# Scan rows loaded two chunks at a time, and output projections by 1024 by 512 quarters, in a hybrid decoder trunk

## Chip, core and metric

The program runs on one core of a Trainium2 chip. The metric is the device time of one launch in microseconds (us): 2238.65 us before, the median of three runs (2238.03 to 2240.89).

## What is computed

A trunk of two residual layers on 1024 tokens of width 1024, all in float32. Layer 0 has two mixers side by side, a Mamba-2 scan in 8 chunks of 128 tokens and differential attention in 8 heads; layer 1 is a gated linear recurrence of 16 heads. Each layer ends in one output projection from 2048 to 1024 that is added to the residual.

```python
# layer 0, in two halves of 1024 channels each
z, xBC, dt, q, k, v, g = split(u @ w_in)
a_cs = cumsum(dt * A)                                   # per head, within a chunk
y_diag = ((C B^T) * exp(segsum(a))) X                   # scores of a chunk, then times X
y_off  = (C prev) * exp(a_cs)                           # what earlier chunks hand on
y = y_diag + y_off + xs * D_skip
y_a = rmsnorm(y * silu(z), ssd_norm_w)
y_b = rmsnorm(diff_attention(q, k, v), subln_w) * silu(g)
h = h + concat(y_a, y_b) @ w_out                        # 2048 x 1024
# layer 1
h = h + (rmsnorm(recurrence(q, k, i, f), norm_w) * silu(g)) @ w_out
out = rmsnorm(h, final_norm_w)
```

## The kernel before

**Numbers.** Every projection multiplies split operands: a value is a rounded part `hi` and the rest `lo`, and three products are summed (hi by hi, hi by lo, lo by hi). So 128 tokens by 1024 inputs take 24 matmuls. `mm_cm` (L174) puts channels on partitions, 128 by 512 outputs each; `mm_tm` (L184) puts tokens on partitions, 128 by 256 outputs each. Weights come in blocks of 1024 rows by 256 columns: `_wprep` loads each half raw (L126, 512 KB into one of two `w_raw` slots), casts it to `w_hi` on ScalarE (L132) and subtracts into `w_lo` on VectorE (L133). There are two slots of each, and a block is prepared while the one before it is in use.

**The scan** (`ssd_steps`) runs in four head groups, woven by hand into the projection pieces of the next group: TensorE's order is as written (`manual_schedule`), that of the other queues is set by a scheduler. A piece is 24 matmuls into one of two `pj` banks: per group eight convolution pieces, evicted by ScalarE alone (L426, L427), and four gate pieces, evicted by a tanh on ScalarE (L232, into the one slot `th`) and a product on VectorE (L233). Per chunk, `first(c)` loads a row tile R (L464: cumulative decays of four heads, 128 columns, broadcast to all partitions; three slots), transposes (L466 to L470), subtracts (L482), exponentiates (L484) and multiplies (L485); `second(c)`, two pieces later, multiplies (L502 to L508) and adds up on VectorE. For `y_off` each pair of chunks loads the same decays again in another layout into the one slot `ey` (L523, two DMAs) and exponentiates them (L525). At each odd chunk, ScalarE squares into `th` (L542) and GpSimd adds from there (L544, L547) before the pair is stored (L548).

**The output projection** (`out_proj`) takes the first 1024 inputs (`ya`), then the second (`yb`). The y tiles come through a raw tile (`w_raw`, `th` or `ey`) and are split from there (`load_y`, L694 to L705). The first half runs over four column blocks of 256, each over all eight token tiles; the second runs over half the tokens with four blocks, and again with the same four, so 12 weight blocks are loaded per layer. Sums are evicted by VectorE (L734, L738, L778), squared on ScalarE (L781), and `finish` normalizes 512 tokens at a time.

SP's queue issues nearly all loads and stores, in order: a DMA whose tile is not free yet holds up what stands behind it.

Of the kernel before, what the change touches and what calls it, by code (L numbers as in the profile page):

```python
# [89 lines left out]
class Net:  # L90
# [23 lines left out]
    def _wprep(self, i):  # L114
# [4 lines left out]
        hi = self.t("w_hi", [P, KT, WB], F32R)  # L119
        lo = self.t("w_lo", [P, KT, WB], F32R)  # L120
        for q in range(2):
            raw = self.t("w_raw", [P, KT // 2, WB])
            k0 = q * (KT // 2)
            o = 0
            for c0, n in cols:
                nc.sync.dma_start(  # L126
                    raw[:, :, o:o + n],
                    src[row0 + k0 * P:row0 + (k0 + KT // 2) * P, c0:c0 + n].rearrange(
                        "(k p) n -> p k n", p=P))
                o += n  # L130
# [48 lines left out]
    def mm_tm(self, out, w, uh, ul, ks=range(KT)):  # L179
        nc = self.nc  # L180
        wh, wl = w
        for k in ks:
            for j, (uu, ww) in enumerate(((uh, wh), (uh, wl), (ul, wh))):
                nc.tensor.matmul(out, lhsT=uu[k], rhs=ww[:, k, :],  # L184
                                 start=(k == 0 and j == 0), stop=(k == KT - 1 and j == 2))
# [20 lines left out]
    def proj_v(self, u):  # L206
        vs = []
        run(self.v_pieces(u, vs))
        return self.v_of(vs)

# [242 lines left out]
def ssd_steps(S, g, tiles, ya, at, lag):  # L453
# [4 lines left out]
    X_, sts, eas = {}, {}, {}  # L458

    def first(c):  # L460
        x0, x1, Bt, Ct = tiles[:4]
        cs = slice(c * P, c * P + P)
        R = S.t(("G", "G", "wT")[(8 * g + c) % 3], [P, 4, P])
        nc.sync.dma_start(R, bc(S.acs_d[hs, cs].unsqueeze(0), [P, 4, P]))  # L464
# [15 lines left out]
        nc.vector.tensor_tensor(cb, pt[:, 384:512], S.triu, op=ALU.mult)  # L480
        for h in range(4):
# [4 lines left out]
        X_[c] = pk, R  # L486

    def second(c):
        Ct = tiles[3]
        cs = slice(c * P, c * P + P)  # L490
        pk, sc = X_[c]
# [26 lines left out]
        if c % 2 == 0:  # L518

            c2 = slice(c * P, (c + 2) * P)  # L520
# [5 lines left out]
            eas[c // 2] = ea, S.t("o", [P, 2, 256])  # L526
        ea, tt = (z[:, :, (c % 2) * P:(c % 2) * P + P] for z in eas[c // 2])
# [5 lines left out]
        if c % 2 == 1:  # L533
            t = eas[c // 2][1]
# [6 lines left out]
            sq = S.t("th", [P, 2, 256])  # L541
# [147 lines left out]
def load_y(S, y_d, wcols, hf, k, tags):  # L689

    nc = S.nc
    n = len(tags)
# [3 lines left out]
    for j in range(n):  # L696
        y = S.t(tags[j], [P, 2, 512], F32R)
        if wcols is not None and k < KT:
            w = wcols[:, k + j:k + j + 1]
            nc.scalar.activation(y[:, 0], raw[:, j], AF.Identity, scale=w)  # L700
            nc.vector.scalar_tensor_tensor(y[:, 1], raw[:, j], w, y[:, 0].bitcast(F32),
                                           op0=ALU.mult, op1=ALU.subtract)
        else:
            nc.scalar.copy(y[:, 0], raw[:, j])
            nc.vector.tensor_tensor(y[:, 1], raw[:, j], y[:, 0].bitcast(F32), op=ALU.subtract)  # L705
# [4 lines left out]
def out_proj(S, y_d, wcols, x_d, x1_tags, rs_a, finish):  # L710
# [3 lines left out]
    part = lambda y, t: [[z[:, i, t * P:t * P + P] for z in y] for i in range(2)]  # L714
    load = lambda hf, k, *tags: load_y(S, y_d, wcols, hf, k, tags)
    ya, yb = [[], []], [[], []]
    for hf in range(2):
        for k in range(0, KT, 2):
            ya[hf] += load(hf, k, "u", "u")
    x1s = [], []  # L720
    for cb in range(4):
        w = S.wnext()
        for hf in range(2):
            x1 = S.t(x1_tags[2 * cb + hf], [P, 4, WB])
            nc.sync.dma_start(x1, x_d[hf * 512:hf * 512 + 512, cb * WB:cb * WB + WB].rearrange(
                "(t p) n -> p t n", p=P))
            x1s[hf].append(x1)
            for t2 in range(2):
                pa = S.ps("pj", [P, 2, WB])
                ts_ = slice(2 * t2, 2 * t2 + 2)  # L730
                for t in range(2):
                    S.mm_tm(pa[:, t], w, *part(ya[hf], 2 * t2 + t))
                if rs_a is None:
                    nc.vector.tensor_tensor(x1[:, ts_], pa, x1[:, ts_], op=ALU.add)  # L734
                else:
                    for t in range(2):
                        tok = hf * 4 + 2 * t2 + t
                        nc.vector.scalar_tensor_tensor(x1[:, 2 * t2 + t], pa[:, t], rs_a[:, tok:tok + 1],  # L738
                                                       x1[:, 2 * t2 + t], op0=ALU.mult, op1=ALU.add)
        if cb == 2:  # L740
            for k in range(KT, 2 * KT - 2, 2):
                yb[0] += load(0, k, "A", "A")
    yb[0] += load(0, 2 * KT - 2, "u")
    ws, pbs = {}, {}

    def block(cb, tag):
        ws[cb] = S.wnext()
        if tag == "pj":
            pbs[cb] = [S.ps("pj", [P, 2, WB]) for _ in range(2)]
        elif tag == "big":  # L750
            pb = S.ps("big", [P, 4, WB])
            pbs[cb] = [pb[:, 0:2], pb[:, 2:4]]

# [441 lines left out]
```

## Time and profile before

| | |
|---|---|
| median of three runs | 2238.65 us |
| the profiled execution | 2242.69 us, its span 2240.9 us |
| TensorE busy in the span | 2178.8 us (97%) |
| VectorE, ScalarE, GpSimd busy | 1269.9, 832.2, 188.8 us |

The page reads so: busy time is the union of an engine's instructions; "idle before" is what the engine waited before an instruction, with the instruction that released it behind "<-". PE is TensorE's matmul side, PEld its weight loads, which overlap it; DVE is VectorE, ACT ScalarE, POOL GpSimd, SPq the queue that SP issues. PEclk is the granted TensorE clock as a share of 2.4 GHz; its other level is 1.2 GHz, shown as 0.50.

### The profile page before, as it was taken

Reading aid. Unit: us, or ns where it says so; the run is one execution under the profiler, and the core shown is the slowest. Engines: PE = TensorE matmul, PEld = TensorE weight load, DVE = VectorE, ACT = ScalarE, POOL = GpSimd, SP = SyncE. Lnnn points to the kernel's source line nnn. Section 1 sums busy time; section 2 is a strip of 40 time slices with the busy share of each in tenths; the row PEclk is TensorE's granted clock in tenths of the full one; section 3 lists DMA queues with packets and bytes.
Section 4 is the critical chain, followed back from the end, with each engine's and each line's share of the span. In section 5 each row is a group of like instructions: output and inputs, shape, how many; then the busy total and the mean of one; then the engine's idle time right before and its main releaser. Section 6 shows DMA issues by size and latency. Waiting matters only on the chain.

```text
span 2240.9 us, 40897 instructions
## 1 busy us (share of the span) xinstructions
PE 2178.8 (97%) x16868; PEld 1920.3 (86%) x16868; DVE 1269.9 (57%) x2864; ACT 832.2 (37%) x1903; POOL 188.8 (8%) x216
## 2 busy tenths in 40 slices
PE   6998998899999999999999999999999999999998
PEld 5787776789898988999988989898989898989998
DVE  4765766565656556755453555555555555557444
ACT  4333333234444545644442323232323222324233
POOL 1001111110000000000010010101010101010000
PEclk9999999999999999999999999999999999999999
DMA  4322233332212221525331111111111111125333
GB/s 138 67 84 66 80 85 81 74 81 64 69 36 67 64 69 41 170 66 159 119 104 39 48 48 48 48 48 48 48 48 48 48 49 48 48 67 165 111 103 122
DMA packets 182256, 169.14 MB, mean 75 GB/s; under 512 B 10239, under 2 KB 163233, under 8 KB 182068
## 3 DMA queue, kind: packets, MB, share of 16 engines
q1 hardware_dynamic: 174564, 152.42, 23.1%
q0 software_dynamic: 3280, 9.90, 2.1%
q10 hardware_dynamic: 4224, 4.19, 0.6%
q8 instruction: 132, 2.16, 0.4%
q14 instruction: 56, 0.46, 0.1%
HBM read 132.66 MB, written 25.43 MB: 71 GB/s over the span
## 4 chain that ended last, share of the span: by engine, by line
PE 51%; DMA 1%; ACT 0%; DVE 0%; issue 0%; POOL 0%; POOLq 0%; ACTq 0%
PE pj L174 24%; PE pj L184 14%; PE big L184 5%; PE big L1051 2%; PE big L1139 1%; PE big L1141 1%; PE s L1128 1%; PE big L1093 1%; PE s L1155 1%; PE s L1122 1%; PE big L1087 0%; PE s L159 0%; DMA ey<-yb 0%; DMA th<-in_lvmask 0%; ACT w_hi L132 0%; DVE w_lo L133 0%
## 5 line engine op out<-in xcount | busy, mean ns | idle before, releaser
L174 PE MATMUL pj<-u,w_hi 128*128 128x512 f32 x3072 | 990.0, 400 | 31.3 <-DVE A L233 21.2
L174 PEld LDWEIGHTS pj<-u,w_hi 128*128 128x128 f32 x3072 | 573.4, 190 | 154.7 <-DVE A L233 23.0
L174 PE MATMUL pj<-u,w_lo 128*128 128x512 f32 x1536 | 607.9, 396 | 0.0
L184 PE MATMUL pj<-w_hi,u 128*128 128x256 f32 x2592 | 492.6, 286 | 1.0 <-DVE A L233 1.0
L184 PEld LDWEIGHTS pj<-w_hi,u 128*128 128x128 f32 x2592 | 409.9, 191 | 3.6 <-DVE A L233 1.4
L184 PE MATMUL pj<-w_lo,u 128*128 128x256 f32 x1296 | 368.3, 284 | 0.0
L174 PEld LDWEIGHTS pj<-u,w_lo 128*128 128x128 f32 x1536 | 291.8, 190 | 61.1 <-issue 0.2
L133 DVE TENSOR_TENSOR w_lo<-w_raw,w_hi 128x1024 fp32r<-128x1024 f32 x168 | 206.3, 1251 | 116.9 <-ACT w_hi L132 116.6
L184 PEld LDWEIGHTS pj<-w_lo,u 128*128 128x128 f32 x1296 | 247.8, 191 | 1.0
L132 ACT CAST w_hi<-w_raw 128x1024 fp32r<-128x1024 f32 x168 | 168.1, 1047 | 188.8 <-PE pj L174 107.6
L233 DVE SCALAR_TENSOR_TENSOR A<-th,pj 128x512 f32<-128x512 f32 x80 | 55.1, 689 | 140.9 <-ACT th L232 140.4
L232 ACT ACTIVATE th<-pj 128x512 f32<-128x512 f32 x96 | 57.2, 596 | 208.5 <-PE pj L174 190.8
L617 ACT ACTIVATE p<-p,mx 128x256 f32<-128x256 f32 (+7 forms) x128 | 98.5, 771 | 72.4 <-DVE mx L613 66.4
L148 POOL TENSOR_TENSOR ro<-rs_t,mhalf 128x4 f32<-128x4 f32 x48 | 52.8, 1100 | 682.4 <-DVE rs_t L147 489.1
L603 PE MATMUL big<-A 128*128 128x512 f32 (+3 forms) x384 | 90.3, 352 | 2.6 <-DMA A<-A 1.3
L968 POOL TENSOR_SCALAR A<-th,fN,fB 128x512 f32<-128x512 f32 x32 | 47.6, 1488 | 470.0 <-ACT th L965 470.0
L637 ACT COPY wT<-s 128x512 f32<-128x512 f32 (+2 forms) x96 | 45.8, 477 | 95.8 <-PE s L635 95.1
L639 PE MATMUL s<-V,wT 128*128 128x128 f32 x576 | 79.7, 275 | 0.6 <-ACT wT L637 0.6
L1035 DVE TENSOR_TENSOR A<-A,p 128x512 f32<-128x512 f32 x96 | 65.8, 686 | 23.5 <-PE big L1051 23.0
L639 PEld LDWEIGHTS s<-V,wT 128*128 128x128 f32 x576 | 74.4, 191 | 3.3 <-ACT wT L637 1.1
L1030 DVE TENSOR_TENSOR p<-p,p 128x512 f32<-128x512 f32 x96 | 66.2, 690 | 15.5 <-PE big L1087 6.2
L603 PEld LDWEIGHTS big<-A 128*128 128x128 f32 x384 | 64.5, 189 | 11.3 <-issue 2.3
(330 smaller groups left out, 2977.1 us busy)
## 6 DMA issues: line engine op xcount, KB each, us to landing
w_raw<-in_even_w_in SPq DMA_DIRECT2D x32, 512.0 KB, 4.7
w_raw<-in_odd_w_in SPq DMA_DIRECT2D x64, 256.0 KB, 3.3
w_raw<-in_odd_w_in SPq DMA_DIRECT2D x32, 512.0 KB, 3.9
w_raw<-in_even_w_in SPq DMA_DIRECT2D x48, 256.0 KB, 4.3
w_raw<-in_even_w_out SPq DMA_DIRECT2D x24, 512.0 KB, 4.4
w_raw<-in_odd_w_out SPq DMA_DIRECT2D x24, 512.0 KB, 4.6
A<-A POOLq DMA_DIRECT2D x32, 256.0 KB, 5.5
yo<-ey SPq DMA_DIRECT2D x32, 256.0 KB, 2.0
```

The source lines that it names most:

```text
L132: nc.scalar.copy(hq, raw)
L133: nc.vector.tensor_tensor(lq, raw, hq.bitcast(F32), op=ALU.subtract)
L148: return nc.gpsimd.tensor_tensor(dst, t[:, :n], self.mhalf[:, :n], op=ALU.pow)
L174: nc.tensor.matmul(out, lhsT=ww[:, k, ms], rhs=uu[k][:, sl], start=(n == 0), stop=(n == 3 * KT - 1))
L184: nc.tensor.matmul(out, lhsT=uu[k], rhs=ww[:, k, :], start=(k == 0 and j == 0), stop=(k == KT - 1 and j == 2))
L232: nc.scalar.activation(th, pj, AF.Tanh, scale=0.5)
L233: nc.vector.scalar_tensor_tensor(out, view(th), 1.0, view(pj), op0=ALU.add, op1=ALU.mult)
L603: nc.tensor.matmul(s[:, k0:k0 + kn], lhsT=q[:, isl], rhs=ks[j][:, k0:k0 + kn], start=(j == 0), stop=(j == 1))
L617: nc.scalar.activation(p[:, :n], p[:, :n], AF.Exp, bias=mx, accum_out=z)
L639: nc.tensor.matmul(po[:, i % 4, :], lhsT=wT[:, j * P:j * P + P], rhs=V(j, hh), start=(j == 0), stop=(j == i))
L1030: nc.vector.tensor_tensor(q, q, bc(t0, [P, L // (2 * h), h]), op=ALU.mult)
L1035: nc.vector.tensor_tensor(k, k, bc(halves(Ts[h], 1)[1], [P, L // (2 * h), h]), op=ALU.mult)
```

## The change

The row tile now holds two chunks (256 columns, three slots), and the load for pair i + 1 is issued in `first` of pair i. The second layout is no longer loaded: `first(c)` exponentiates half the heads on each half of the partitions straight from the row tile into `ey` or `cm` (by the chunk's parity), before the subtraction overwrites the rows. The squares go into the chunk's own tile (`p0` or `bt`) in place of `th`. A weight block may now be 512 rows by 512 columns, and the projection runs over quarters of 1024 by 512: two blocks (kq 0 and 1) of 512 rows each, all eight token tiles, sums of 128 by 512. Both weight slots are then in use at once; in the first and the last pair of token tiles the order is kq 0 of both tiles, then kq 1 of both. Eight blocks are loaded per layer. y tiles are loaded into their own second half and split in place.

```diff
+    def rows_load(self, i):
+        if i < 16:
+            g, q = divmod(i, 4)
+            self.rows[i] = self.t(("G", "G", "wT")[i % 3], [P, 4, 256])
+            self.nc.sync.dma_start(self.rows[i], bc(
+                self.acs_d[4 * g:4 * g + 4, q * 256:q * 256 + 256].unsqueeze(0), [P, 4, 256]))
...
     def first(c):
-        R = S.t(("G", "G", "wT")[(8 * g + c) % 3], [P, 4, P])
-        nc.sync.dma_start(R, bc(S.acs_d[hs, cs].unsqueeze(0), [P, 4, P]))
+        if c % 2 == 0:
+            S.rows_load(4 * g + c // 2 + 1)
+        R = S.rows[4 * g + c // 2][:, :, (c % 2) * P:(c % 2) * P + P]
...
+        ea = S.t(("ey", "cm")[c % 2], [P, 2, P])
+        for hh in range(2):
+            nc.scalar.activation(ea[64 * hh:64 * hh + 64], R[64 * hh:64 * hh + 64, hh::2], AF.Exp)
...
     def second(c):
-            ea = S.t("ey", [P, 2, 256])
-            for hh in range(2):
-                nc.sync.dma_start(ea[64 * hh:64 * hh + 64],
-                                  bc(S.acs_d[4 * g + hh:4 * g + 4:2, c2].unsqueeze(0), [64, 2, 256]))
-            nc.scalar.activation(ea, ea, AF.Exp)
...
-            sq = S.t("th", [P, 2, 256])
+            sq = pk[:, 0:512].rearrange("p (b t) -> p b t", b=2)
             nc.scalar.activation(sq, t, AF.Square)
...
 def load_y(S, y_d, wcols, hf, k, tags):
-    raw = S.t("w_raw" if n == 2 else (("th", "ey")[k % 2] if hf else "th"), [P, n, 512])
-    nc.sync.dma_start(raw, y_d(k, n)[:, :, hf * 512:hf * 512 + 512].rearrange("b p t -> p b t"))
+    for j, tag in enumerate(tags):
+        y = S.t(tag, [P, 2, 512], F32R)
+        raw = y[:, 1].bitcast(F32)
+        nc.sync.dma_start(raw, y_d(k + j, 1)[0, :, hf * 512:hf * 512 + 512])
...
 def out_proj(S, y_d, wcols, x_d, x1_tags, rs_a, finish):
+    def pair():
+        i = S.wpos
+        S.wpos += 2
+        S._wprep(i)
+        S._wprep(i + 1)
+        return S.wtiles[i], S.wtiles[i + 1]
+
+    def sums(ws, ys):
+        for t in range(0, NT, 2):
+            pas = [S.ps("pj") for _ in range(2)]
+            order = ((0, 0), (1, 0), (0, 1), (1, 1)) if t in (0, NT - 2) else ((0, 0), (0, 1), (1, 0), (1, 1))
+            for j, kq in order:
+                hf, tt = divmod(t + j, 4)
+                y = ys[hf][4 * kq:4 * kq + 4]
+                S.mm_tm(pas[j], ws[kq], *([z[:, i, tt * P:tt * P + P] for z in y] for i in range(2)),
+                        first=kq == 0, last=kq == 1)
+                if t == NT - 2 and j == 1:
+                    S._wprep(S.wpos + kq)
+                if kq == 1:
+                    yield hf, tt, pas[j]
...
+    for n in range(2):
+        ws = pair()
+        rss = []
+        for hf, t, pa in sums(ws, late):
...
+            xr = x1s[hf, n, t // 2][:, t % 2]
+            nc.vector.tensor_tensor(xr, pa, xr, op=ALU.add)
+            jk = S.t("ey", [P, 512])
+            nc.scalar.activation(jk, xr, AF.Square, accum_out=ss[hf][:, t, n:n + 1])
...
-    out = lambda w: [(w, half * D, [(cb * WB, WB)]) for half in (0, 1, 1) for cb in range(4)]
+    out = lambda w: [(w, kq * 512, [(n * 512, 512)])
+                     for half in (0, 2) for n in range(2) for kq in (half, half + 1)]
```

The scheduler moves what stands around these edits. Three places follow, in the order in which a queue issues; the line numbers are those of each kernel, and a number behind a tile's name tells its copies apart.

**SP's queue early in the scan's first group.** The row loads are L464 before (128 columns) and L219 after (256), the second layout is L523, the store of a finished pair L548 and L558, and L126 and L128 load weights. Before:

```order
L464 DMA G_1258<-acs_d_552 128x4x128
L523 DMA ey_1212<-acs_d_552 64x2x256 x2
L548 DMA ya_74<-o_1049 128x2x256
L464 DMA wT_1335<-acs_d_552 128x4x128
L464 DMA G_1427<-acs_d_552 128x4x128
```

After:

```order
L219 DMA G_1259<-acs_d_552 128x4x256
L558 DMA ya_74<-o_1051 128x2x256
L219 DMA G_1427<-acs_d_552 128x4x256
L128 DMA w_raw_1513<-in_even_w_in 128x4x128 x2
L128 DMA w_raw_1518<-in_even_w_in 128x4x128 x2
L558 DMA ya_74<-o_1217 128x2x256
```

Between two stores of `ya` stood two row loads and two loads of the other layout, the next chunk's rows among them; now one load stands there, for the pair after.

**ScalarE's queue at the first two gate pieces of that group.** The gate's tanh is L232 before and L243 after, the squares L542 and L552, the exponential of the rows L484 and L501, that of the other layout L525 and L497. Before:

```order
L484 ACTIVATE G<-G 128x512
L525 ACTIVATE ey<-ey 128x512
L479 COPY bt<-s_1337 128x128
L438 ACTIVATE p_1255<-A 128x1024
L542 ACTIVATE th<-o 128x512
L232 ACTIVATE th<-pj 128x512 x2
```

After:

```order
L497 ACTIVATE cm<-wT 64x256 x2
L243 ACTIVATE th<-pj 128x512
L501 ACTIVATE wT<-wT 128x4x128
L492 COPY bt<-s_1338 128x128
L449 ACTIVATE p_1256<-A 128x1024
L243 ACTIVATE th<-pj 128x512
L552 ACTIVATE p_1166<-o 128x512
```

Both gate pieces stood behind the squares; now both stand ahead of them.

**VectorE's queue where layer 1's projection passes to its last weight blocks.** The addition of a sum is L778 before and L782 after, the product with the norm's weights L990 and L997, the subtraction for `w_lo` L133 and L135. Before:

```order
L133 TENSOR_TENSOR w_lo_21319<-w_raw_21324,w_hi_21318 128x1024
L778 TENSOR_TENSOR A_20616<-big_21338,A_20616 128x512
L990 TENSOR_TENSOR A_20402<-A_20402,o_20110 128x512
L990 TENSOR_TENSOR A_20616<-A_20616,o_20112 128x512
L778 TENSOR_TENSOR A_20616<-big_21338,A_20616 128x512
L133 TENSOR_TENSOR w_lo_21448<-w_raw_21449,w_hi_21447 128x1024
```

After:

```order
L782 TENSOR_TENSOR A_19518<-pj_20020,A_19518 128x512
L135 TENSOR_TENSOR w_lo_20047<-w_raw_20048,w_hi_20046 128x1024
L135 TENSOR_TENSOR w_lo_20047<-w_raw_20052,w_hi_20046 128x1024
L997 TENSOR_TENSOR A_19518<-A_19518,o_19230 128x512
L782 TENSOR_TENSOR A_19518<-pj_20021,A_19518 128x512
L997 TENSOR_TENSOR A_19518<-A_19518,o_19230 128x512
L135 TENSOR_TENSOR w_lo_20085<-w_raw_20086,w_hi_20084 128x1024
L135 TENSOR_TENSOR w_lo_20085<-w_raw_20090,w_hi_20084 128x1024
```

One block was prepared between two additions of the block before it; now two blocks are prepared around the last two additions (A_19518) of the quarter before.

## Rows read from the trace of the kernel before


**Rows 1.** The page, busy time by engine: us (share of the span) and instructions.

```profile
PE 2178.8 (97%) x16868; PEld 1920.3 (86%) x16868; DVE 1269.9 (57%) x2864; ACT 832.2 (37%) x1903; POOL 188.8 (8%) x216
```

**Rows 2.** Windows: stretch, its us, busy of PE, PEld, DVE, ACT, POOL (count), PEclk, DMA share, GB/s.

```profile
0.00:100.00 100.00, 83.19 (x388) 63.23 (x389) 60.69 (x113) 43.98 (x70) 10.87 (x23) 1.00 0.41 110
100.00:440.00 340.00, 310.27 (x1611) 252.70 (x1610) 214.38 (x440) 115.26 (x192) 40.02 (x50) 0.95 0.30 78
```

**Rows 3.** Windows inside the scan, same columns: where the clock falls.

```profile
160.00:200.00 40.00, 34.00 (x158) 27.20 (x155) 28.26 (x56) 13.14 (x21) 4.28 (x5) 0.91 0.32 86
...
260.00:300.00 40.00, 32.95 (x150) 25.95 (x149) 22.98 (x49) 9.90 (x16) 6.26 (x6) 0.87 0.25 71
...
360.00:420.00 60.00, 44.57 (x216) 35.63 (x214) 28.81 (x67) 15.52 (x26) 8.18 (x9) 0.89 0.24 58
```

**Rows 4.** PE's waits from 100 to 440: waiter, releaser, total, times, longest.

```profile
PE pj L174 <- DVE A L233: 21.2, 7, 5.6
PE pj L174 <- DVE A L570: 8.0, 1, 8.0
```

**Rows 5.** Timeline at a group's first gate piece: start, us, what, [idle before <-releaser].

```profile
266.46 0.61 ACT L542 ACTIVATE th<-o 128x512 f32<-128x512 f32 x1
...
267.15 2.44 POOL L547 TENSOR_TENSOR V<-V,th 128x256 f32<-128x256 f32 x2 [3.83 <-ACT th L542]
...
269.62 0.60 ACT L232 ACTIVATE th<-pj 128x512 f32<-128x512 f32 x1 [2.55 <-POOL V L547]
270.25 0.69 DVE L233 SCALAR_TENSOR_TENSOR A<-th,pj 128x512 f32<-128x512 f32 x1 [0.91 <-ACT th L232]
...
271.00 1.22 PE L174 MATMUL pj<-u,w_hi 128*128 128x512 f32 x2 [5.23 <-DVE A L233]
```

**Rows 6.** Who waited for the loads L464 and L523: us in total, times.

```profile
  DVE G L482: 34.1, 16
  DVE wT L482: 18.7, 8
...
  ACT ey L525: 60.3, 16
```

**Rows 7.** The costliest instructions by form: total, mean ns, idle before and its releasers.

```profile
L569 ACT ACTIVATE A<-pj 64x512 fp32r<-64x512 f32 x64 | 37.4, 589 | 53.7 <-PE pj L174 27.7 <-DVE A L570 22.1 <-DVE o L537 2.4
```

**Rows 8.** TensorE's timeline in projections: two 512-wide, then two 256-wide matmuls.

```profile
113.41 0.39 PE L174 MATMUL pj<-u,w_lo 128*128 128x512 f32 x1
...
117.49 0.39 PE L174 MATMUL pj<-u,w_lo 128*128 128x512 f32 x1
...
2120.39 0.28 PE L184 MATMUL pj<-w_lo,u 128*128 128x256 f32 x1
...
2125.79 0.28 PE L184 MATMUL pj<-w_lo,u 128*128 128x256 f32 x1
```

**Rows 9.** The page's costliest groups: the two steps that prepare weights.

```profile
L133 DVE TENSOR_TENSOR w_lo<-w_raw,w_hi 128x1024 fp32r<-128x1024 f32 x168 | 206.3, 1251 | 116.9 <-ACT w_hi L132 116.6
L132 ACT CAST w_hi<-w_raw 128x1024 fp32r<-128x1024 f32 x168 | 168.1, 1047 | 188.8 <-PE pj L174 107.6
```

**Rows 10.** DMA issues, the page's and those from 2040 to 2200: KB, us to landing.

```profile
w_raw<-in_odd_w_out SPq DMA_DIRECT2D x24, 512.0 KB, 4.6
...
th<-yo SPq DMA_DIRECT2D x6, 256.0 KB, 2.6
```

**Rows 11.** PE's waits from 880 to 1200, at the handover of a weight block.

```profile
PE big L184 <- DVE bt L778: 1.2, 1, 1.2
```

**Rows 12.** Timeline where the scan ends and attention begins; L590 loads masks.

```profile
472.92 4.72 SPq L590 DMA_DIRECT2D ph<-tz_d  x8
...
475.50 0.42 DVE L529 TENSOR_TENSOR o<-big,ey 128x256 f32<-128x256 f32 x1 [0.58 <-PE big L508]
...
481.46 0.29 DVE L607 CUSTOM_DVE_ANT_0 p<-big,cm 128x128 f32<-128x128 f32 x1 [3.49 <-PE big L603]
```

**Rows 13.** Timeline at layer 1's projection: its first matmul; last addition of a sum.

```profile
2027.47 0.28 PE L184 MATMUL pj<-w_hi,u 128*128 128x256 f32 x1
...
2233.82 0.42 DVE L778 TENSOR_TENSOR bt<-pj,bt 128x256 f32<-128x256 f32 x1
```

More of the change, by code (lines that the diff above doesn't have):

```diff
@@ L118, in _wprep @@
         src, row0, cols = self.wspecs[i]
-        hi = self.t("w_hi", [P, KT, WB], F32R)
-        lo = self.t("w_lo", [P, KT, WB], F32R)
+        wid = sum(n for _, n in cols)
+        kt = KT * WB // wid
+        hi = self.t("w_hi", [P, kt, wid], F32R)
+        lo = self.t("w_lo", [P, kt, wid], F32R)
         for q in range(2):
-            raw = self.t("w_raw", [P, KT // 2, WB])
-            k0 = q * (KT // 2)
+            raw = self.t("w_raw", [P, kt // 2, wid])
+            k0 = q * (kt // 2)
             o = 0
@@ L176, in mm_cm, with mm_tm @@
                 n += 1
-    def mm_tm(self, out, w, uh, ul, ks=range(KT)):
+    def mm_tm(self, out, w, uh, ul, first=True, last=True):
         nc = self.nc
         wh, wl = w
-        for k in ks:
+        kt = len(uh)
+        for k in range(kt):
             for j, (uu, ww) in enumerate(((uh, wh), (uh, wl), (ul, wh))):
                 nc.tensor.matmul(out, lhsT=uu[k], rhs=ww[:, k, :],
-                                 start=(k == 0 and j == 0), stop=(k == KT - 1 and j == 2))
+                                 start=(first and k == 0 and j == 0), stop=(last and k == kt - 1 and j == 2))
     def v_pieces(self, u, vs):
@@ L518, in second @@
         if c % 2 == 0:
[L520 to L527 removed]
+            ts[c // 2] = S.t("o", [P, 2, 256])
+        tt = ts[c // 2][:, :, (c % 2) * P:(c % 2) * P + P]
         if c:
@@ L717, in out_proj @@
+    y = [[], []]
     for hf in range(2):
         for k in range(0, KT, 2):
[L719 to L742, printed above, removed]
@@ new lines, in out_proj @@
+            y[hf] += load(hf, k, "u", "u")
+        if hf == 0:
+            ws = pair()
+    x1s = {}
+    tags = iter(x1_tags)
+    late = [[], []]
+    for n in range(2):
+        if n:
+            ws = pair()
+        for hf, t, pa in sums(ws, y):
+            if t % 2 == 0:
+                x1 = x1s[hf, n, t // 2] = S.t(next(tags), [P, 2, 512])
+                r0 = hf * 512 + t * P
+                nc.sync.dma_start(x1, x_d[r0:r0 + 256, n * 512:n * 512 + 512].rearrange("(t p) n -> p t n", p=P))
+            if rs_a is None:
+                nc.vector.tensor_tensor(x1[:, t % 2], pa, x1[:, t % 2], op=ALU.add)
+            else:
+                nc.vector.scalar_tensor_tensor(x1[:, t % 2], pa, rs_a[:, hf * 4 + t:hf * 4 + t + 1], x1[:, t % 2],
+                                               op0=ALU.mult, op1=ALU.add)
+            if n == 1 and t % 2 == 1:
+                k = 4 * hf + t - 1
+                late[0] += load(0, KT + k, *(("A", "A") if k < 6 else ("u", "u")))
@@ new lines, in out_proj @@
+    tags1 = "V", "V", "G", "G", "p0", "p0", "p1", "wT"
+    ss = [S.sm.tile([P, 4, 2], F32, name="ss4", bufs=2) for _ in range(2)]
+    for n in range(2):
+        ws = pair()
+        rss = []
+        for hf, t, pa in sums(ws, late):
+            if n == 0 and hf == 0:
+                for k in (2 * t, 2 * t + 1):
+                    late[1] += load(1, KT + k, tags1[k])
+            xr = x1s[hf, n, t // 2][:, t % 2]
+            nc.vector.tensor_tensor(xr, pa, xr, op=ALU.add)
+            jk = S.t("ey", [P, 512])
+            nc.scalar.activation(jk, xr, AF.Square, accum_out=ss[hf][:, t, n:n + 1])
+            if n == 0:
+                finish.early(xr)
+                continue
@@ L795, in out_proj @@
             rss.append(rs)
-        finish(hf, x1s[hf], rss)
+            finish.row(hf, t, [x1s[hf, m, t // 2][:, t % 2] for m in range(2)], rs)
+            if t == 3:
+                finish(hf, x1s, rss)
+                rss = []
 def wspecs(a):
@@ L879, in finish @@
                 S.u_block(u, k, hf, [xn[t // 2][:, t % 2, j * P:j * P + P] for t in range(4)], wcol[:, k:k + 1])
-    finish.early = None
+    finish.early = lambda xr: None
+    finish.row = lambda hf, t, x1, rs: None
     return finish
@@ L892, in layer0 @@
         setup_rest(S)
+    S.rows = {}
+    S.rows_load(0)
     S.ysq = S.t("V", [P, L])
```

113 lines of the change are left out of this document (31 added, 82 removed).

## Prediction, made before the changed kernel ran

> **What bounds the kernel now.** I read the page's busy times first: TensorE is busy for 97% of the span, every other engine for 57% or less [rows 1]. So time can be won in two ways only: from TensorE's idle time, 2240.9 − 2178.8 = 62.1 us, or by making its work shorter. A step added to another engine costs something only where TensorE then waits for it.
>
> Next, the busy time by stretch shows where the idle time is. The start holds 16.8 us, which the change doesn't touch, and the scan, 100 to 440, holds 29.7 [rows 2]. Inside the scan three windows hold 6.0, 7.05 and 15.4 us, together 28.5, and there the granted clock is 0.91, 0.87 and 0.89 [rows 3]: after the longer stalls TensorE runs for a while at 1.2 GHz. Busy time times (1 − clock) is what that costs: 3.1 + 4.3 + 4.9 = 12.2 us. So 28.5 + 12.2 = 40.7 us can be had from the scan.
>
> TensorE's waits name the releasers: the gate product L233, seven times, 21.2 us; and L570, once, 8.0 us, an eviction of the first attention piece, in the last group [rows 4]. The timeline shows the chain of one of the three longest: the squares L542 write `th`, GpSimd's two additions hold it until 269.6, only then can the gate's tanh use the one `th`, then the product, and TensorE goes on after 5.23 us [rows 5]. These three first-gate stalls make up 14.9 of the 21.2 us. Three more, at third gates, are 5.6 us together; there VectorE itself was late, since its subtraction L482 waited for a row load. Such waits sum to 34.1 + 18.7 = 52.8 us on VectorE, and ScalarE waits 60.3 us for the second layout [rows 6].
>
> **The scan.** The squares go to the chunk's own tile, so the tanh no longer waits for GpSimd: in the new order two gate pieces stand ahead of the squares. That removes 14.9 us. The row loads are issued a pair ahead, about three projection pieces, against a landing within one, so VectorE's and ScalarE's waits go, and with them the third-gate stalls, 5.6. The 8.0 us stall mixes two causes, a late row load and a queue of evictions on VectorE; I take half, 4.0. Together 24.5 of the 28.5 us, and the clock's share with them: 12.2 × 24.5 / 28.5 = 10.5. That makes 35.
>
> What is added: two exponentials a chunk on 64 partitions. The nearest row is L569, half the partitions of 512 columns, 0.589 us [rows 7]; half as many columns each make 0.3 to 0.59, and I take 0.4. Over 32 chunks that is 26 us of ScalarE, against the 16 removed exponentials; ScalarE is busy for a third of this stretch [rows 2], so it is covered, unless it delays the chain of one chunk: the subtraction now waits for both exponentials. `ey` and `cm` have one slot each, and a chunk tile is held until GpSimd has added from it. I take 4 us for these hops, from 0 to 14 by rows 5 (one GpSimd hold of 2.44 us in some six places). The scan gives **−31** (−40.7 to −21).
>
> `cm` also holds the attention masks of head 0. Before, these were loaded early; now they must wait for the last chunk's product, which reads `cm` and starts at 475.5. Eight issues take 4.7 us on SP, and the first mask is used at 481.5 [rows 12]. 475.9 + 4.7 and a landing (2.6 us for a larger load [rows 10]) give 483.2, up to 1.7 us late for VectorE; TensorE has gate pieces to run there. I take **+0.5** (0 to 3).
>
> **The output projections.** TensorE's timeline gives the pitch: from 2120.39 to 2125.79 lie 45 matmuls of 256 columns, 0.1200 us each; from 113.41 to 117.49 lie 18 of 512 columns, 0.2267 us each [rows 8]. Two layers need 3072 of the narrow ones (8 token tiles × 16 inputs of 128 × 3 products × 4 column blocks × 2), 368.6 us; or 1536 wide ones, 348.2 us. This gives **−20.5** (−20.5 to 0).
>
> The Trainium skill speaks against this gain: TensorE: Matmul & The Clock Gate, section "Wait — 56ns, not 53.3ns?", puts the pitch at N/2.4 GHz plus about 2.5 ns. By it 256 columns would take 109.2 ns and 512 columns 215.8, an estimate of 4 us for the whole change. The trace disagrees in both (120.0 and 226.7 ns), so the sum goes by the trace.
>
> **The handover of weight blocks.** Before, a block was prepared while the other was in use, with one wait of 1.2 us in the stretch around layer 0's projection [rows 11]: **−1.2**. Now both slots belong to the quarter in use. Take S as the end of a quarter. Its kq 0 slot is free 24 × 0.2267 = 5.4 us before S, since both last tiles do kq 0 first. The raw halves wait ready; a cast takes 1.05 us and a subtraction 1.25 [rows 9], so the raw slots are free at S − 3.1 and S − 1.9. The halves of the next kq 1 load in 4.6 us [rows 10] to S + 1.5 and S + 2.7, and cast and subtraction bring them to S + 3.8 and S + 5.1. They are needed at S + 5.4 and S + 6.8: 1.6 us to spare. But in VectorE's new order additions and norm products stand among these subtractions, and an addition ahead of them waits until S − 2.7 for the seventh tile's sum and takes 0.7 (512 columns, as L233 in rows 5). Then they end at S − 0.8 and S + 0.5, 2.4 later, and the handover is 2.4 − 1.6 = 0.8 us late. Six handovers (three a layer) at 1 us are **+6** (0 to 32, six times 0.8 plus one load of 4.6 that SP holds back).
>
> **y loads.** They now go into their own `u` slots, which layer 1's last projection piece frees as it goes, from about 5.7 us ahead of the first product at 2027.47 [rows 13]. Issue, landing 2.6 [rows 10], rounding and subtraction make about 4.3 us, and a tile lands faster than its six wide products run (1.36 us): covered, with 1.4 us to spare; **+0.5** (0 to 3). In layer 0 an attention head lies between, which covers it all.
>
> **The tail.** The last sum is 512 wide instead of 256 (the narrow addition takes 0.42 us [rows 13]), with fewer steps behind it: **+0.3** (−1 to 1). Between the layers the first half's norm has four tiles of 5.4 us to run beside, 21.8 us, against some 14 us of work on each of two engines: nothing.
>
> **Sum:** −31 + 0.5 − 20.5 − 1.2 + 6 + 0.5 + 0.3 = −45.4 us. The profiled execution took 2242.69 us (span and 1.8 around it), 4.0 over the median; taken from it the sum gives 2197.3, taken from the median 2193.3, which I forecast.
>
> **Rivals.**
>
> (1) VectorE's backlog, not `th`, holds the gate pieces: the tanh is early, but the product L233 still queues behind the chunks' work. Then 14.9 us and their clock share, 14.9 / 28.5 × 12.2 = 6.4, stay: 2193.3 + 21.3 = 2214.6. For it: the third-gate stalls are of this kind. Against: in rows 5 the product followed the tanh at once.
>
> (2) The handover is late by a whole load: 5.4 us six times, 32.4 in place of 6: 2219.7. For it: a weight load stands behind other loads on SP, and two raw slots are all there is. Against: fewer weights are loaded in all.
>
> (3) Slower: the scan's chunks now hang on ScalarE, with two exponentials ahead of the subtraction and one slot each for `ey` and `cm`. If TensorE, which takes its work in a fixed order, waits 2 us for the scores of each of 32 chunks, that is +64: 2257.3. It decides from 45.4 / 32 = 1.4 us a chunk. Against: two pieces of 5.4 us lie between a chunk's start and its use of the scores, and of the waits in rows 4 none is on them.
>
> (4) The wide matmul brings nothing, with a pitch of 0.24 us: 2193.3 + 20.5 = 2213.8. Against: rows 8, at the same type and size. By the skill's pitch, above, it would be an estimate of 2193.3 + 16.5 = 2209.8.
>
> **How the numbers follow.** The forecast has 0.67, (1) 0.13, (2) 0.08, (4) 0.03, (3) 0.05; the rest, 0.04, is a mixture that ends within 0.2% (4.5 us), which is about what a measurement of this kernel can tell from no change. Faster is all but the last two: 0.91, same 0.04, slower 0.05. The best case, all 40.7 us and no late handover, is −40.7 − 20.5 − 1.2 = −62.4, 2176.3; the range begins at 2177 and ends at 2220, at rival (2).
>
> **What would show it.** Right: from 100 to 440 TensorE idles under 6 us at a clock of 0.99 or more; no wait of VectorE for `acs_d`, none of a tanh for GpSimd; 512-wide matmuls of the projection at 0.227 us; waits for `w_lo` of about 1 us at six places. The forecast is wrong if the clock still falls in the scan, if one handover costs over 3 us, or if new waits for the exponentials of the rows show up ahead of L482's successor.

## The result, and the profile after

The changed kernel takes 2206.8 us (median of four runs, 2204.8 to 2209.8) against 2239.8 beside it: the ratio is 0.9852, 95% interval 0.9834 to 0.9869. That is 33.0 us less, inside the range and the way that was forecast, but a quarter short of the 45.4 that the sum had. The profiled execution took 2206.88 us, its span 2205.1, which is 35.8 less than the span before. (The profiled execution before, 2242.69 us, lay 2.9 over the median beside it, so differences between the two profiles come out a little too large.)

The first line is the page's busy time; the windows under it repeat [rows 2] and [rows 3] for the kernel after (columns as there).

```profile
PE 2154.8 (98%) x15332; PEld 1832.8 (83%) x15332; DVE 1245.9 (57%) x2816; ACT 826.2 (37%) x1863; POOL 192.5 (9%) x216
```

```profile
0.00:100.00 100.00, 83.90 (x393) 63.95 (x394) 61.89 (x116) 44.34 (x71) 11.61 (x24) 1.00 0.41 114
100.00:440.00 340.00, 331.36 (x1813) 272.59 (x1812) 228.74 (x486) 142.65 (x254) 46.73 (x58) 0.99 0.30 75
```

```profile
160.00:200.00 40.00, 39.44 (x210) 31.95 (x208) 27.70 (x66) 15.97 (x30) 3.44 (x5) 1.00 0.32 90
...
260.00:300.00 40.00, 39.16 (x206) 31.53 (x205) 25.23 (x55) 19.06 (x33) 4.78 (x7) 1.00 0.30 71
...
360.00:420.00 60.00, 53.61 (x376) 47.41 (x372) 32.50 (x83) 21.72 (x43) 9.43 (x14) 0.94 0.24 58
```

In the scan the first two windows have lost their idle time (0.6 and 0.8 us are left of 6.0 and 7.05) and the granted clock is 1.00 there, its level of 2.4 GHz; only the last, in the fourth group, still idles 6.4 us at 0.94. TensorE's waits from 100 to 440 say what is left, to be read against [rows 4]: above all the first attention piece, L580.

```profile
PE pj L176 <- DVE A L580: 6.4, 1, 6.4
PE pj L176 <- DVE A L244: 1.7, 3, 0.6
```

Where the rest of the 33 us came from, and where it didn't, shows in windows cut at the same events in each kernel: head 0's first score matmul, the first matmul of layer 1's input projection, and the last one of that kind. The fourth cut lies at a late matmul of the output projection and differs by form, so the last two lines are read as one. First the kernel before, then the one after.

```profile
0.00:481.00 481.00, 434.46 (x2257) 350.80 (x2258) 297.32 (x608) 169.18 (x279) 58.47 (x84) 0.97 0.33 86
481.00:1140.80 659.80, 653.58 (x4421) 602.18 (x4420) 383.46 (x1117) 322.89 (x787) 38.67 (x55) 1.00 0.30 85
1140.80:2027.20 886.40, 885.38 (x8283) 764.18 (x8282) 479.88 (x938) 265.89 (x656) 81.16 (x62) 1.00 0.16 49
2027.20:2224.90 197.70, 196.62 (x1841) 194.57 (x1841) 102.41 (x180) 67.70 (x162) 8.34 (x11) 1.00 0.40 131
2224.90:2240.90 16.00, 8.76 (x74) 8.55 (x72) 6.86 (x22) 6.59 (x20) 2.16 (x4) 0.85 0.33 133
```

```profile
0.00:449.00 449.00, 424.26 (x2257) 344.07 (x2257) 293.84 (x609) 189.52 (x328) 59.81 (x84) 0.99 0.32 83
449.00:1110.20 661.20, 648.11 (x3649) 562.16 (x3649) 370.28 (x1085) 308.57 (x743) 38.38 (x54) 0.99 0.28 78
1110.20:1998.10 887.90, 886.38 (x8288) 764.93 (x8287) 481.12 (x942) 267.27 (x659) 81.72 (x63) 1.00 0.17 51
1998.10:2196.30 198.20, 195.33 (x1142) 161.34 (x1141) 98.27 (x177) 58.67 (x131) 11.52 (x13) 1.00 0.32 108
2196.30:2205.10 8.80, 0.72 (x4) 0.26 (x2) 2.42 (x5) 2.17 (x4) 1.08 (x2) 0.73 0.30 119
```

The scan gave 481.0 − 449.0 = 32.0 us. With the same number of matmuls up to that cut, TensorE's idle time fell by 21.8 us (46.5 to 24.7) and its busy time by 10.2 (434.5 to 424.3), as the clock rose from 0.97 to 0.99. Layer 0's attention and projection, which should have given about 10, took 1.4 more. Layer 1's body took 1.5 more, and its projection with the tail gave 213.7 − 207.0 = 6.7. So the scan's gain is there, and the projections are what fell short, above all in layer 0. The pitch isn't the reason: from 2100.06 to 2108.90 TensorE's timeline in layer 1's projection has 39 steps of one wide matmul, 0.2267 us each, as in [rows 8].

```profile
2100.06 0.39 PE L187 MATMUL pj<-w_lo,u 128*128 128x512 f32 x1
...
2108.90 0.39 PE L187 MATMUL pj<-w_lo,u 128*128 128x512 f32 x1
```

### The profile page after: what moved, and what is told of

It reads as the page before. It is cut to its first block, busy times and chain, and to the rows that moved or that the text cites. A ratio compares the mean times of both kernels' runs of the same rounds, so it can differ in the third digit from the quotient of the medians.

```text
span 2205.1 us, 37628 instructions
## 1 busy us (share of the span) xinstructions
PE 2154.8 (98%) x15332; PEld 1832.8 (83%) x15332; DVE 1245.9 (57%) x2816; ACT 826.2 (37%) x1863; POOL 192.5 (9%) x216
## 4 chain that ended last, share of the span: by engine, by line
PE 93%; DVE 2%; DMA 2%; ACT 1%; issue 1%; SPq 0%; POOLq 0%; POOL 0%; ACTq 0%; DVEq 0%
PE pj L176 48%; PE pj L187 26%; PE big L613 3%; PE s L649 2%; PE big L1054 2%; PE big L1142 1%; PE s L645 1%; PE big L1144 1%; PE s L1131 1%; PE big L525 1%; PE big L1096 1%; PE s L1158 1%; PE s L161 1%; DMA A<-in_x 1%; PE big L519 1%
## 5 line engine op out<-in xcount | busy, mean ns | idle before, releaser
L187 PE MATMUL pj<-w_hi,u 128*128 128x256 f32 (+1 forms) x2112 | 479.5, 316 | 3.9 <-DVE rr L631 1.8
L187 PEld LDWEIGHTS pj<-w_hi,u 128*128 128x128 f32 x2112 | 351.4, 191 | 28.2 <-issue 2.0
L187 PE MATMUL pj<-w_lo,u 128*128 128x256 f32 (+1 forms) x1056 | 332.4, 315 | 0.5 <-DVE w_lo L135 0.5
L135 DVE TENSOR_TENSOR w_lo<-w_raw,w_hi 128x1024 fp32r<-128x1024 f32 x152 | 185.8, 1245 | 130.3 <-ACT w_hi L134 130.0
L134 ACT CAST w_hi<-w_raw 128x1024 fp32r<-128x1024 f32 x152 | 152.6, 1048 | 165.0 <-PE pj L176 111.6
L187 PEld LDWEIGHTS pj<-w_lo,u 128*128 128x128 f32 x1056 | 201.5, 191 | 12.5 <-DVE w_lo L135 1.4
L243 ACT ACTIVATE th<-pj 128x512 f32<-128x512 f32 x96 | 57.2, 596 | 197.2 <-PE pj L176 196.9
L649 PE MATMUL s<-V,wT 128*128 128x128 f32 x576 | 80.4, 277 | 2.2 <-ACT wT L647 2.2
L649 PEld LDWEIGHTS s<-V,wT 128*128 128x128 f32 x576 | 75.8, 192 | 6.3 <-ACT wT L647 2.7
L647 ACT COPY wT<-s 128x512 f32<-128x512 f32 (+2 forms) x96 | 45.9, 479 | 93.5 <-PE s L645 92.7
L446 DVE SCALAR_TENSOR_TENSOR A<-V,convw,A 128x1023 f32<-128x1023 f32 (+2 forms) x48 | 61.6, 1286 | 22.9 <-ACT A L438 22.8
```

Of the source, the lines that this page charges most:

```text
L187: nc.tensor.matmul(out, lhsT=uu[k], rhs=ww[:, k, :], start=(first and k == 0 and j == 0), stop=(last and k == kt - 1 and j == 2))
L243: nc.scalar.activation(th, pj, AF.Tanh, scale=0.5)
L446: nc.vector.scalar_tensor_tensor(cv[:, d:], rp[:, :L - d], S.convw[:, k, ci:ci + 1], cv[:, d:], op0=ALU.mult, op1=ALU.add)
L649: nc.tensor.matmul(po[:, i % 4, :], lhsT=wT[:, j * P:j * P + P], rhs=V(j, hh), start=(j == 0), stop=(j == i))
```

## Experiments: which part gives what

Two kernels hold one part of the change each, without more edits: the scan's hunks, or the projections' hunks.

> The kernel before with the scan part of the change alone (rows two chunks ahead, no second layout, squares in the chunk's tile); projections as before. Between the two profiles the first score matmul of head 0 moved from 481.0 to 449.0 us, so if the scan gains what stands ahead of that point, this kernel takes 2239.8 - 32 = 2208, and the projections bring almost nothing. Rival: the prediction's 15 us of the projections are there in full and the scan is worth the rest of the 33 us, 18; then it takes 2222.

Measured: 2211.1 us (2209.9 to 2211.4), ratio 0.9867 (0.9842 to 0.9892), so 29.3 us less than before.

> The kernel before with the projection part alone (quarters of 1024 by 512, y in place), the scan as before. Theory: layer 1 gains about 8 us, layer 0 gives its 10 us back in TensorE's waits and the tail costs 2, so 2239.8 - 5 = 2235. Rival: the projections gain 15 us and the two parts get in each other's way only when together: 2225.

Measured: 2239.1 us, ratio 0.9994 (0.9981 to 1.0008): with the old scan the projections bring nothing that can be told from zero, and the 5 us expected didn't come either. Its stages repeat the picture: layer 0 takes 663.3 us in place of 659.8, layer 1's projection with the tail 206.6 in place of 213.7. On top of the new scan the projections are worth 2211.1 − 2206.8 = 4.3, with runs that spread by 1.6 and 5 us. The rival in both expectations, 15 us for the projections, falls.

The scan's two edits were then taken apart, on the kernel with the scan part alone and on the one before:

```diff
-            sq = pk[:, 0:512].rearrange("p (b t) -> p b t", b=2)
+            sq = S.t("th", [P, 2, 256])
```

> The scan part without the squares' move: rows two chunks ahead, both exponentials from them, squares still in th. By the prediction's steps the first-gate stalls stay (14.9 us and 6.4 of the clock): the scan part alone took 2211, so 2232; the third-gate stalls and the half of the 8 us stall are gone. Rival: VectorE's late rows also make the squares late, and the rows bring most of it: 2215.

Measured: 2222.6 us against 2238.5, 15.9 less (ratio 0.9927, 0.9910 to 0.9943), between the expectation and its rival. So the move of the squares is worth 2222.6 − 2211.1 = 11.5 us where the rows come early.

```diff
-            sq = S.t("th", [P, 2, 256])
+            sq = X_[c][0][:, 0:512].rearrange("p (b t) -> p b t", b=2)
```

> The kernel before with the squares in the chunk's tile alone, row loads as before. By the prediction's steps this takes the first-gate stalls away, 14.9 + 6.4 = 21.3 us: 2240 - 21 = 2219. Rival: without the early rows the product of the gate still comes late behind VectorE's wait for the rows, and it gains less than 8: 2232 or more.

Measured: 2216.9 us, 21.6 less (0.9902, 0.9887 to 0.9916), where the prediction's step gives 21.3; its rival, 2232 or more, falls. TensorE's waits from 100 to 450 in these two, rows alone and then squares alone:

```profile
PE pj L174 <- DVE A L241: 10.1, 6, 3.2
PE pj L174 <- DVE A L577: 6.4, 1, 6.4
```

```profile
PE pj L174 <- DVE A L570: 8.0, 1, 8.0
PE pj L174 <- DVE A L233: 4.9, 4, 1.7
```

The squares' move takes the three long stalls away without the early rows; what it leaves is mostly the third-gate stalls, in all 4.9 us, and the 8.0. The early rows take the third-gate stalls from 5.6 to 1.7 us, and shorten the first-gate stalls too, from 14.9 to 8.5: in the stall of [rows 5] the squares began 0.7 us after TensorE had stopped, with the early rows 1.7 us ahead of its stop. The hold of `th` stays. So the first-gate stalls had both causes, and the parts overlap: 15.9 + 21.6 = 37.5 apart, 29.3 together. The long stall at L570 (L577, L580) is 8.0 us with the late rows and 6.4 with the early ones, in every run.

## Experiments: what layer 0 gives back

Against the run with the scan part alone, the changed kernel's layer 0 should take 10.2 us less between the first score and layer 1; its stage took 658.5 there and takes 661.2. So 12.9 us went missing. The stage in that run:

```profile
449.40:1107.90 658.50, 653.73 (x4423) 602.32 (x4423) 384.22 (x1117) 322.30 (x786) 38.77 (x55) 1.00 0.31 85
```

Of the 12.9 us, 8.3 are idle time of TensorE (13.1 against 4.8). These stages spread between kernels whose code in them is the same: layer 0 in the old form takes 657.3 to 660.1 us in five profiles, layer 1's projection with its tail in the new form 205.5 to 208.7 in six; stage differences under 3 us there say little. Three causes stood against each other: the y loads in place (A), the handover between quarters (B), and head 7's chain (C, D).

The first pair of runs exchanges the y loads: back through raw tiles under the new quarters, and in place under the old blocks.

```diff
-        raw = y[:, 1].bitcast(F32)
-        nc.sync.dma_start(raw, y_d(k + j, 1)[0, :, hf * 512:hf * 512 + 512])
+    raw = S.t("w_raw" if n == 2 else (("th", "ey")[k % 2] if hf else "th"), [P, n, 512])
+    nc.sync.dma_start(raw, y_d(k, n)[:, :, hf * 512:hf * 512 + 512].rearrange("b p t -> p b t"))
```

> The changed kernel, but the y tiles come through a raw tile again (w_raw for pairs, th and ey for single ones) as before, while the quarters stay. Theory A: layer 0's gain was lost to the y loads in place, because a load can start only when its own slot is free and then its rounding and subtraction hold up attention's work and evictions in the queues of ScalarE and VectorE; then 5 to 8 us come back, 2199 to 2202, and the waits of TensorE from 870 to 1030 shrink. Rival B: the coarse quarters with two blocks in use at once lose it at the handover; then 2206 or more, since w_raw is now shared by weights and y.

Measured: 2217.9 us, 11 slower than the changed kernel: A's 2199 to 2202 didn't come, and the time lies on B's side. But the waits name another reason. In the second half of layer 0's projection TensorE waits 7.7 us once for a single y tile that comes through `th` or `ey`, and layer 1's projection with its tail takes 211.5 us in place of 207.0. That says that the single tiles are better in place, and settles neither A nor B.

> The scan part of the change and the y loads in place, but the old blocks of 1024 by 256. Theory A: the loads in place cost 5 to 8 us against the run with the scan part alone: about 2214. Rival B: within 2 us of that run, about 2208.

Measured: 2216.9 us, 5.9 more than the scan part alone: loads in place cost that much under the old blocks. Of the stages, layer 0 took 664.1 in place of 658.5. Here A holds. It shows where layer 0's first y tiles arrive, first in this run and then in the one with the scan part alone (windows, columns as before): 3.1 us of idle time, and a clock of 0.89 and 0.94 that costs about as much again.

```profile
860.00:880.00 20.00, 16.85 (x98) 14.93 (x97) 13.98 (x31) 15.09 (x27) 1.03 (x2) 0.89 0.83 254
880.00:900.00 20.00, 20.00 (x153) 19.64 (x152) 14.15 (x51) 9.56 (x31) 1.04 (x1) 0.94 0.51 127
```

```profile
860.00:880.00 20.00, 20.00 (x136) 18.24 (x136) 12.54 (x31) 12.39 (x25) 1.03 (x2) 1.00 0.53 139
880.00:900.00 20.00, 19.95 (x158) 19.14 (x157) 18.14 (x60) 12.90 (x34) 1.03 (x1) 1.00 0.77 242
```

How it happens shows in 13 us of the same stretch, in the changed kernel and then in the one with the scan part alone:

```profile
871.00:884.00 13.00, 10.06 (x57) 8.01 (x56) 12.65 (x26) 12.26 (x24) 1.03 (x2) 0.95 1.11 312
```

```profile
871.00:884.00 13.00, 12.95 (x105) 12.53 (x105) 9.67 (x30) 9.03 (x24) 1.03 (x2) 1.00 0.86 225
```

In place, the 16 loads are issued one behind another, from 863.3 on within 9.6 us, and their roundings begin within 14.7 us (866.3 to 881.0); through the raw slots that takes 24.4 us (863.7 to 888.1). VectorE and ScalarE are busy for nearly all of the 13 us, and TensorE idles 2.9 of it. ScalarE's timeline of the changed kernel has ten roundings L709, and behind them the copies of attention (L647) that TensorE's products L649 need (the last line is TensorE's):

```profile
874.28 2.55 ACT L709 ACTIVATE u<-u,cols 128x512 fp32r<-128x512 f32 x4
876.73 0.57 ACT L647 COPY wT<-s 128x512 f32<-128x512 f32 x1
877.20 1.95 ACT L709 ACTIVATE u<-u,cols 128x512 fp32r<-128x512 f32 x3
...
879.79 1.95 ACT L709 ACTIVATE u<-u,cols 128x512 fp32r<-128x512 f32 x3
881.76 0.58 ACT L647 COPY wT<-s 128x512 f32<-128x512 f32 x1
...
882.40 1.77 PE L649 MATMUL s<-V,wT 128*128 128x128 f32 x8 [1.56 <-ACT wT L647]
```

Before, two raw slots let two pairs in at a time. The next two runs put that pacing back: for all pairs, then for layer 0's first 16 tiles alone.

```diff
+    if n == 2:
+        raws = S.t("w_raw", [P, n, 512])
+        nc.sync.dma_start(raws, y_d(k, n)[:, :, hf * 512:hf * 512 + 512].rearrange("b p t -> p b t"))
```

> The changed kernel, but the y tiles that are loaded in pairs (all of the first half's 16, and the second half's first 8) come through w_raw again; the single ones stay in place. Theory A: what layer 0 loses is the burst of the first 16 loads in place, whose roundings and subtractions pile up ahead of attention's copies; with pairs paced by two raw slots 4 to 6 us come back: 2201 to 2203. Rival B: the raw slots are needed for two weight blocks a quarter, so sharing them with y costs more than the burst: 2208 to 2214.

Measured: 2206.2 us, no change, and so between A (2201 to 2203) and B (2208 to 2214). But the stages moved against each other: layer 0 took 655.5 (5.7 less than in the changed kernel), layer 1's projection with its tail 211.3 (4.3 more).

> The changed kernel, but layer 0's first 16 y tiles alone come through w_raw again, in pairs; all others stay in place. Theory A: the burst of those 16 is what the loads in place cost in layer 0 (the run with all pairs staged took 655.5 us from the first score to layer 1, the changed kernel 661.2), and layer 1 keeps its loads in place: 2206.8 - 5.7 = 2201. Rival B: what that run won in layer 0 came from the second half's tiles, whose roundings no longer waited for a late load in ScalarE's queue: then this one gains under 2, 2205 or more.

Measured: 2205.7 us (2203.6 to 2206.7), 1.1 less than the changed kernel, with layer 0's stage at 656.6, 4.6 less, in the profiled run. The 13 us from 871 to 884 have lost their idle time there:

```profile
871.00:884.00 13.00, 12.71 (x75) 11.02 (x74) 9.22 (x24) 7.42 (x14) 1.03 (x2) 1.00 0.80 228
```

So the burst is gone, as A has it. But the time, over 2205, is on rival B's side. In the profile, stages that the edit doesn't touch took some of the gain: the scan 450.2 us in place of 449.0, layer 1's projection with its tail 208.7 in place of 207.0. So what the burst costs under the quarters stays open between the 1 us of the medians, which runs that spread by 3 us can't tell from none, and the 5 us of the stage.

Cause B, the handover. At the end of the first quarter TensorE waits 1.8 us, and the chain is not the one predicted: the sum's eviction L767, which frees the bank for the next quarter, stands on VectorE behind the weights' subtraction L135 and a y tile's L713. TensorE's row names the small step behind the eviction, which isn't an operand here; the eviction itself ended at 941.92 (VectorE's timeline, then TensorE's):

```profile
939.45 1.21 DVE L135 TENSOR_TENSOR w_lo<-w_raw,w_hi 128x1024 fp32r<-128x1024 f32 x1
940.58 0.69 DVE L713 TENSOR_TENSOR A<-A 128x512 fp32r<-128x512 f32 x1
941.18 0.74 DVE L767 SCALAR_TENSOR_TENSOR A<-pj,rsa,A 128x512 f32<-128x512 f32 x1
```

```profile
942.07 0.47 PE L187 MATMUL pj<-w_hi,u 128*128 128x512 f32 x1 [1.83 <-DVE rr L631]
```

Waits for `w_lo` itself sum to 0.5 us in layer 0, and in layer 1 no wait of the projection stands in the list at all. One run asked whether the order of the half sums is what covers them:

```diff
-            order = ((0, 0), (1, 0), (0, 1), (1, 1)) if t in (0, NT - 2) else ((0, 0), (0, 1), (1, 0), (1, 1))
+            order = (0, 0), (0, 1), (1, 0), (1, 1)
```

> The changed kernel with the plain order of the four half sums everywhere (each tile's kq 0, then its kq 1), so that a kq 0 slot is free 2.7 us before a quarter's end in place of 5.4, and kq 1 is needed 2.7 us after the next one's start in place of 5.4. If the handover has no slack, as the prediction has it, each of six costs 5.4 us more: 2235 to 2239. Rival: the profile after shows waits for w_lo of 0.3 us or less at the handovers, so that some slack is there; the six then cost 2 us or less each, 2207 to 2219.

Measured: 2203.0, 2207.4 and 2211.6 us, and a fourth execution of 4331 for which nothing here shows a reason. The first expectation is out. In the profiled execution, the one of 2211.6, layer 0's waits for `w_lo` sum to 2.4 us in place of 0.5, so the order does cover some there; by the times, its worth stays open within 5 us to either side of nothing.

Cause C. From 984.6 to 1000.4 no projection matmul runs in the changed kernel; TensorE has head 7's last steps alone, with two waits (TensorE's timeline):

```profile
984.59 0.39 PE L187 MATMUL pj<-w_hi,u 128*128 128x512 f32 x1
...
994.34 0.66 PE L645 MATMUL s<-ident,p 128*128 128x128 f32 x4 [1.04 <-DVE p L634]
996.92 0.44 PE L645 MATMUL s<-ident,p 128*128 128x128 f32 x2 [1.92 <-ACT wT L647]
...
1000.37 0.50 PE L187 MATMUL pj<-w_hi,u 128*128 128x512 f32 x1 [0.30 <-DVE A L767]
```

The projection goes on once a sum is evicted, into a residual tile whose slot head 7 had held. So the run with the first 16 tiles staged was changed once more: four residual loads of layer 0's second quarter are moved ahead of the second half's y tiles, to that quarter's first sum:

```diff
+            if first:
+                for f in first:
+                    x1_load(*f)
```

> As the run with layer 0's first 16 y tiles staged, and the four residual tiles of layer 0's second quarter get their slots before the y tiles of the second half. Theory C: from 985 to 1000 no projection matmul runs, because the sums of the second quarter wait for residual tiles whose A slots stand behind six y tiles and head 7's keys; with slots of their own the projection fills that gap, and 3 to 5 us come back, idle and clock: 2196 to 2198. Rival: the rest of head 7 then runs bare a little later, and it comes to the same, 2201.

Measured: 2203.4 us, 2.3 less than the run it is built on and 3.4 less than the changed kernel; with the last run below it is the fastest that computes everything. But C's 2196 to 2198 didn't come, and layer 0's stage didn't get shorter (658.2 against 656.6). The gap without projection matmuls didn't close: it moved to 992.9 to 1006.6, and TensorE waited 2.9 us for a y tile and 2.4 for head 7. That is as the rival has it. In the profiles the gain lies in layer 1's projection with its tail (205.7 us against 208.7), which the edit doesn't touch, so the 2.3 us aren't shown to be its work.

Cause D, the strong form: the first half of the projection is only filler.

```diff
+                if j == 1 and not three:
+                    continue
```

> The changed kernel with one of the three products (hi of y by lo of the weights) left out in layer 0's first quarter: 64 wide matmuls fewer, 14.5 us of TensorE. Theory D: the first half of layer 0's projection only fills TensorE beside head 7, whose dependent steps and the store and load of its y set when the second half can start; then most of these 14.5 us turn into idle time before the end of head 7, and the kernel gains 5 us or less: 2202 or more. Rival: TensorE's work is the bound there and what the change lost in layer 0 lies in single stalls: then it gains 12 to 14.5 us, 2192 to 2195.

This kernel leaves out one of the three products there. Measured: 2196.8 us, 10.0 less than the changed kernel by the medians, between the theory and its rival. Layer 0's stage shrank by 8.8 of the 14.5 us taken out. Of the other 5.7, 1.9 are more idle time in the stage (15.0 us against 13.1), and the rest is busy time that didn't shrink, for the most part at a lower clock beside head 7 (windows of that run, then of the changed kernel):

```profile
860.00:1000.00 140.00, 129.64 (x670) 108.20 (x670) 90.22 (x270) 69.37 (x172) 7.11 (x9) 0.96 0.39 116
```

```profile
860.00:1000.00 140.00, 131.53 (x695) 110.83 (x693) 83.29 (x252) 65.50 (x164) 6.21 (x8) 0.99 0.35 104
```

So work saved ahead of the end of head 7 reaches the end for six to seven tenths, by the stage and by the medians. D falls as the whole cause and stands as a part.

Last, each layer's projection in the form that suits it: layer 0's out of the kernel before, layer 1's as changed.

> The scan part of the change, layer 0's projection as before (blocks of 1024 by 256, y through raw tiles), layer 1's projection as changed. By the stages of the profiles (layer 0's attention and projection: 658.5 us with the old form, 661.2 with the new; layer 1's projection and tail: 213.8 and 207.0) this is 2.7 us faster than the changed kernel: 2204. Rival: the loss in layer 0 is made by something else than its projection, and then the 10.2 us of shorter matmuls are missed: 2217.

Measured: 2203.8 us (2203.2 to 2204.7), ratio 0.9844 (0.9829 to 0.9858), as expected: 3.0 less than the changed kernel by the medians. The intervals overlap, and layer 0's stage, 659.9 in place of 661.2, is within what such stages spread. Layer 1's body is back at 886.4 from 887.9; every kernel with layer 0's projection in quarters has 887.5 to 888.1 there and every one in the old form 886.3 or 886.4, so those 1.5 us came from how layer 0 ends. So layer 0's half of the projections' change showed no gain, by the medians a loss of 3.0 us, and layer 1's half gained 2211.1 − 2203.8 = 7.3 of the 10.2 that the pitch makes for a layer.

## Why the prediction was right, and where not

**The scan** was right in size and in kind: −30.5 forecast with the masks' term, −29.3 measured alone. By the profiles it is 21.8 us of idle time and 10.2 of the clock, where the working has 24.5 less 4 and 10.5. The hold of `th` was priced at 21.3 and measured 21.6 by itself. That the total fits so well is in part luck: the 8.0 us stall kept 6.4 (I gave it 4, and the late row made 1.6 of it, not half), and the 4 us set aside for new hops weren't needed, so these two errors cancelled. Nor were the first-gate stalls the work of `th` alone: the early rows by themselves take 6.4 of their 14.9 us. Here rival (1), a backlog on VectorE, had its sign; but with the squares moved nothing of it was left. Rival (3) didn't show: ScalarE's two exponentials made no wait of TensorE, and the masks of head 0 none either.

**The signs** named beforehand came out mixed. VectorE waits for no row load from 100 to 440 and no tanh waits for GpSimd. But TensorE idles 8.6 us there and not under 6, the clock still falls in the fourth group, and new waits for the rows' exponentials did show up ahead of the subtraction (VectorE's waits from 100 to 440):

```profile
DVE G L499 <- ACT ey L497: 4.3, 2, 3.9
```

The first two are mostly the stall of 6.4 us; the third held up no matmul that shows in TensorE's waits.

**The pitch** was right: 0.2267 us, which makes the 20.5 for TensorE's own work and leaves nothing of rival (4). By the rule of the Trainium skill (TensorE: Matmul & The Clock Gate, section "Wait — 56ns, not 53.3ns?") the wide form would have given 4 us, an estimate, and 4.3 came out. The trace doesn't bear that out: its steps are 0.2267 us, so the two figures agree by chance, and what is missing was lost elsewhere.

**The handover** was put at +6 and cost about 2.3 in layer 0 and nothing in layer 1. Its working was for the wrong wait: the blocks are there in time (waits for `w_lo` of about 1 us at six places were expected, and they sum to 0.5), and what was late, once, is the eviction of a last sum behind the next block's subtraction. Rival (2), a whole load late six times, falls with it.

**The y loads** are the step that failed most clearly. I wrote that in layer 0 an attention head lies between, "which covers it all", and took nothing for it (the 0.5 us were layer 1's). The head doesn't cover them; it is what they delay. Under the old blocks they cost 5.9 us, under the quarters somewhere from 1 to 5. I had asked only whether the tiles are there in time, and not what their roundings and subtractions stand in front of: they come in a burst, in two queues that TensorE waits for.

**Hidden gain.** The sum took all of the pitch's 20.5 us. Layer 0's first half, 5.1 of them, runs beside head 7, and by the shortened quarter's stage about four tenths of such work, an estimate of 2 us, are lost to idle time and a lower clock.

**The ends.** Layer 1's body took 1.5 us more, where I had nothing. The tail was put at +0.3 and took 0.9: from the end of the last matmul at 2197.0 to 2205.1 are 8.1 us, before it was 7.2. Waits like the one of [rows 11] are still there (1.2 and 0.6 us for L782), so the −1.2 didn't come either (in layer 0; layer 1's projection has none).

The sum had −14.9 us for the projections. Added up from what the runs showed: −20.5 + 5.9 + 2.3 + 2.0 + 1.5 + 0.9 = −7.9, against −4.3 measured. Some 3.6 us remain, and over 8 if the y loads cost only 1 under the quarters. In layer 0's stage TensorE was busy for 648.1 us against 653.7 in the run with the scan part alone, 5.6 less where the pitch makes 10.2. Of the other 4.6, the granted clock accounts for 1.4 (busy time times one less the clock, summed over the stage in steps of 5 us, is 2.9 us against 1.5); the other 3.2 have no cause that these runs show. So the scan's share of the account is shown, and the projections' is shown only in part.

## What to carry to other kernels

Work taken off TensorE counts in full only where nothing else paces the stage: next to a chain of small dependent steps, here one attention head, three to four tenths of it were lost. A staging buffer also paces: without it loads arrive in a burst, and their conversions fill in-order queues in front of the steps that the bound engine needs; so ask of each removed buffer what it held back. And a shared one-slot temporary, here `th`, which ScalarE writes for two purposes and both VectorE and GpSimd read, can cost more than its busy time shows: one line was worth 21.6 us by itself, and 11.5 after the row loads had been moved.

## What the runs showed of the hardware

Sixteen loads of 256 KB issued one behind another within 9.6 us landed 5.7 us after issue (median), while up to 418 GB/s were moved; six such loads in a quieter stretch took 2.6 us [rows 10]. Two weight loads of 512 KB issued behind that burst took 9.6 us in place of 4.6:

```profile
u<-ya SPq DMA_DIRECT2D x16, 256.0 KB, 5.7
w_raw<-in_even_w_out SPq DMA_DIRECT2D x2, 512.0 KB, 9.6
```

I had put the landing of a y tile at 2.6 us, from that quieter stretch; in the burst it is twice that. (DMA issues of the changed kernel from 860 to 880, us to landing.)
